# The tanh and last product of each convolution unit, issued behind the next unit's evictions

## The chip, the cores and the metric

The kernel runs on one core of a Trainium2 chip. A core has a matrix engine (TensorE, PE in the profile), three engines for elementwise work (VectorE or DVE, ScalarE or ACT, GpSimd or POOL) and SyncE (SP), which here only issues loads. Each engine works through its own list of instructions in order; an instruction whose input isn't there yet holds everything behind it on that engine. Matmul results land in PSUM, a small memory of eight buffers here, and another engine must read a result out (evict it) before the buffer can be used again. The metric is the time of one execution in microseconds (us) on the device; the median of several is compared.

## The reference

A trunk of two layers over x (1, 256, 1024). Each layer normalises x, multiplies it by one wide input matrix, feeds three token mixers (a Mamba-2 scan, attention over a sliding window, forgetting attention), projects each back to 1024, adds them with sigmoid gates, multiplies by an output matrix and adds x.

```python
for layer in range(DEPTH):                     # 2
    h = rms_norm(x, norm_w[layer])
    proj = einsum('bsd,de->bse', h, w_in[layer])        # 1024 x 12832
    (a_xbc, a_z, a_dt, b_q, b_k, b_v, b_z,
     c_q, c_k, c_v, c_f, c_z, gates) = split(proj, ...)
    y_a = mamba2_branch(a_xbc, a_z, a_dt, conv_w[layer], conv_b[layer], ...)
    y_b = sliding_window_branch(b_q, b_k, b_v, b_z, sinks[layer], cos, sin)
    y_c = forgetting_attention_branch(c_q, c_k, c_v, c_f, c_z, f_bias[layer])
    branch = einsum('bsiw,iwd->bsid', stack([y_a, y_b, y_c], axis=2), w_proj[layer])
    g = sigmoid(gates + gate_bias[layer])
    x = x + einsum('bsd,de->bse', sum(g * branch, axis=2), w_out[layer])
return rms_norm(x, final_norm_w)
```

The change touches the first lines of the Mamba-2 branch, a causal convolution of width 4 over each of 2048 channels by itself, followed by silu:

```python
xbc = silu(causal_depthwise_conv(a_xbc, conv_w, conv_b))
xs, bm, cm = split(xbc, [1024, 1536])          # inputs, B and C of the scan
```

## The kernel before

**Products.** Every large product is made in three: activations and weights are each split into a high and a low half, and hi·hi, lo·hi and hi·lo are summed in PSUM. Weights stream in over SyncE's DMA queue into six raw buffers (`load_part`, L331), ScalarE copies the high half out (L261) and VectorE subtracts it for the low half (L262). At most four split parts are held at a time, and a new part is split when an old one is released. So both engines have this stream of splits (276 of each in the kernel) beside everything else.

**Units.** The program is a list of operations, worked through one after the other. A unit is 24 matmuls into one of three PSUM buffers named mm: `chan` makes 128 channels x 256 tokens (24 matmuls, 128x256 each), `tok` 128 tokens x up to 512 columns. Five more PSUM buffers (mx) serve attention, scan and transposes. When a unit is done, its eviction reads the buffer; a later unit's first matmul needs the buffer that was evicted three units before.

**The convolution units.** `u_conv` (L672 to L694) handles 128 channels, unit u of 16: 8 to 11 are B, 12 to 15 are C, 0 to 7 are xs. ScalarE evicts the product twice, a plain copy to x_ (L682) and a scaled copy with bias to a (L683). VectorE adds the three shifted taps onto a (L686, 255, 254 and 253 wide). ScalarE then makes the tanh of a (L689), and VectorE the last product (th + 1) * a (L690), which by the scaling of the weights is the silu. After units 1, 3, 5 and 7 a group of the scan (`ssd_group`, L696) is queued. So a ScalarE instruction (the tanh) waits for VectorE's taps, and a VectorE instruction (the last product) for that tanh, within each unit.

**The order around it.** In each layer, the sixteen conv units come in pairs, 8 and 9 first, then up to 15, then 0 to 7, with other units between the pairs. Layer 0: gate-path units of the sliding-window branch (`u_z`, tanh L770, product L773) behind 9, 11 and 15; two gate units (`u_gate`, bias added L894, tanh L895) behind 3; behind 5 the *late split*, `split_late`, which splits the attention result times its gate path into the halves (L261 and L262) that the attention projection multiplies; and that projection's first units behind 7. Layer 1: `u_z` behind 9, 13 and 15, the two gate units behind 1, and behind 5 the late split directly followed by the projection. Between units, `pump` starts steps of what is queued (attention: scores and softmax L542, exp L548, L554 to L560, transposed probabilities L577; the scan: DMA of cumulated decays L701, L707, L714, L717, taps of the decay L724, their exps L726 and L730, L731, state L737, decay times scores L742), each with a due time on a clock that counts only matmuls.

PE's order is thus fixed by the program. VectorE, ScalarE and GpSimd get theirs in this part from a scheduler, which mostly keeps the order in which the program issues, and moves an instruction where it expects another to be ready sooner. Tiles of 128x256 (tag L1) have fourteen buffers.

Of the kernel before, what the change touches and what calls it, by code (L numbers as in the profile page):

```python
# [13 lines left out]
AF = mybir.ActivationFunctionType  # L14
ALU = mybir.AluOpType

P = 128
S = 256
# [7 lines left out]
D_K, D_Q, D_QK, D_G0, D_FOX, D_BDMA, D_BIAS = 6.0, 5.5, 2.0, 8.0, 0.0, 4.0, 2.0  # L26
# [18 lines left out]
def hybrid_trunk(  # L45
# [14 lines left out]
                bias=2, st=2, sm=6)  # L60
    count = [0]

    def T(tag, shape, dtype=F32, bufs=None):
        count[0] += 1
        return sb.tile(shape, dtype, tag=tag, name=f"{tag}_{count[0]}",
                       bufs=bufs if bufs is not None else BUFS.get(tag, 1))
# [8 lines left out]
    def pmx():  # L75
        return PS("mx", 5)

    act = nc.scalar.activation
    stt = nc.vector.scalar_tensor_tensor
# [19 lines left out]
    def transpose(o, a, i):  # L99
        clock["t"] += 0.109  # L100
        nc.tensor.transpose(o, a, i)  # L101

    def launch(br, gen, delay=0.0):
        clock["n"] += 1
        waiting.append([clock["t"] + delay, clock["n"], br, gen, None])
# [145 lines left out]
    def halves(ap):  # L251

        return ap.rearrange("p (a i) -> p a i", a=2)
# [142 lines left out]
    for l in range(L):  # L396
        y = Layer()
# [274 lines left out]
    def u_conv(y, u, c):  # L672
        def f(w):
            p = chan(y, w, c)
            if u == 8:
                y.bcT = T("L8", [P, 8, S])
            if u == 0:
                y.xs = T("L8", [P, 8, S])
            dst = y.xs[:, u, :] if u < 8 else y.bcT[:, u - 8, :]
            a = T("L1", [P, S])  # L680
            x_ = T("L1", [P, S])
            act(halves(x_), p, AF.Copy)  # L682
            act(halves(a), p, AF.Identity, scale=y.vec[:, 48 + u:49 + u], bias=y.vec[:, 64 + u:65 + u])  # L683
            for j in (2, 1, 0):
                s = 3 - j
                stt(a[:, s:S], x_[:, 0:S - s], y.vec[:, 16 * j + u:16 * j + u + 1], a[:, s:S],  # L686
                    op0=ALU.mult, op1=ALU.add)
            th = T("L1", [P, S])
            act(th, a, AF.Tanh)  # L689
            stt(dst, th, 1.0, a, op0=ALU.add, op1=ALU.mult)  # L690
            if u < 8 and u % 2 == 1:
                launch(0, ssd_group(y, u // 2), D_G0)
            pump()
        return f  # L694

    def ssd_group(y, g):  # L696
        yield lambda: not any(m[2] == 1 for m in waiting)
        yield "ssd"
        xdt = T("L2", [P, 2, 256])
        bcg = T("L4", [P, 4, S])  # L700
        nc.scalar.dma_start(bcg, y.cumd[4 * g:4 * g + 4, 0, :].partition_broadcast(P))  # L701
        hs = slice(4 * g, 4 * g + 4)
        for t in range(2):
            p = pmx()
            for j in range(2):
                transpose(p[:, j * P:(j + 1) * P], y.xs[:, 2 * g + j, t * P:(t + 1) * P], ident)
            tt(xdt[:, t, :].rearrange("p (h d) -> p h d", h=4),  # L707
               p[:, 0:256].rearrange("p (h d) -> p h d", h=4), bc(y.dt[:, t, hs], 2, 64), op=ALU.mult)
        p = pmx()
        transpose(p[:, 0:P], y.bcT[:, g, 0:P], ident)  # L710
        bt = T("bt", [P, P])
        act(bt, p[:, 0:P], AF.Copy)
        ds = T("ds", [P, 4], bufs=2)
        tt(ds, bcg[:, :, P - 1], y.acum[:, 0, hs], op=ALU.subtract)  # L714
        act(ds, ds, AF.Exp)
        xds = T("L1", [P, 256])
        tt(xds.rearrange("p (h d) -> p h d", h=4), xdt[:, 0, :].rearrange("p (h d) -> p h d", h=4),  # L717
           bc(ds, 2, 64), op=ALU.mult)
        decs = []
        for c in range(2):  # L720
            tk = slice(c * P, (c + 1) * P)
            dec = T("L2", [P, 4, P])
            for h in range(4):
                stt(dec[:, h, :], bcg[:, h, tk], y.acum[:, c, 4 * g + h:4 * g + h + 1], negtri,  # L724
                    op0=ALU.subtract, op1=ALU.add)
            act(dec, dec, AF.Exp)  # L726
            decs.append(dec)

        cx = T("L2", [P, 4, P])
        act(cx, bcg[:, :, P:S], AF.Exp)  # L730
        tt(cx, cx, bc(y.bcT[:, 4 + g, P:S], 1, 4), op=ALU.mult)  # L731
        yield D_SSD

        p = pmx()
        mm(p[:, 0:256], bt, xds, start=True, stop=True)
        st = T("st", [P, 256])
        act(st, p[:, 0:256], AF.Copy)  # L737
        for c in range(2):
            tk = slice(c * P, (c + 1) * P)
            p = pmx()  # L740
            mm(p[:, 0:P], y.bcT[:, g, tk], y.bcT[:, 4 + g, tk], start=True, stop=True)
            tt(decs[c], decs[c], bc(p[:, 0:P], 1, 4), op=ALU.mult)  # L742
        yield D_SSD2
        for c in range(2):
            tk = slice(c * P, (c + 1) * P)
            for j in range(2):
                u = 2 * g + j
                py = pmx()
                for s in range(c + 1):
                    for i in range(2):  # L750
                        h = 2 * j + i
                        hc = slice(64 * h, 64 * h + 64)
                        a, b = (xdt[:, c, hc], decs[c][:, h, :]) if s == 0 else (st[:, hc], cx[:, h, :])
                        mm(py[64 * i:64 * i + 64, 0:P], a, b, start=(s == 0), stop=(s == c))
                stt(y.xs[:, u, tk], y.xs[:, u, tk], y.dsk[:, u:u + 1], py[:, 0:P],
                    op0=ALU.mult, op1=ALU.add)
        yield D_EVAC
        tokens["ssd"] += 1


    def u_z(y, br, u, c):
        def f(w):
            p = chan(y, w, c)
            if u == 0 and br != 0:
                y.sz[br] = T("L8", [P, NK, S])
            if u == 0 and br == 0:
                y.yh[br] = T("L8", [P, 2, NK, P], F32R)
                y.yl[br] = T("L8", [P, 2, NK, P], F32R)
            th = T("L1", [P, S])
            act(halves(th), p, AF.Tanh, scale=0.5)  # L770
            y.zdone.add((br, u))
            if br != 0:
                stt(halves(y.sz[br][:, u, :]), halves(th), 1.0, p, op0=ALU.add, op1=ALU.mult)  # L773
            else:
                drain(0)
                sz = T("L1", [P, S])
                stt(halves(sz), halves(th), 1.0, p, op0=ALU.add, op1=ALU.mult)
                tt(y.xs[:, u, :], y.xs[:, u, :], sz, op=ALU.mult)
                sq = T("L1", [P, S])
                act(sq, y.xs[:, u, :], AF.Square)  # L780
                y.sq.append(sq)
                if u % 2 == 1:
                    tt(y.sq[-2], y.sq[-2], y.sq[-1], op=ALU.add)
                    launch(3 if u < 4 else 4, group_norm(y, u // 2, y.sq[-2]), D_GN1)
            pump()
        return f
# [28 lines left out]
    def u_cv(y, c, t, i=None):  # L815

        def f(w):
            p = tok(y.hTh, y.hTl, w, t)
            if y.cv is None:
                y.cv = T("L8", [P, 2, D])  # L820
            m = w.n if i is None else w.n - 16
            rn = 1.0 if y.rn is None else y.rn[:, t:t + 1]
            if i is None:
                act(halves(y.cv[:, t, c:c + m]), p, AF.Copy, scale=rn)
            else:
                n = w.n // 2
                act(y.cv[:, t, c:c + n], p[:, 0, :], AF.Copy, scale=rn)
                act(y.cv[:, t, c + n:c + m], p[:, 1, 0:m - n], AF.Copy, scale=rn)
                logits(y, t, i, p[:, 1, m - n:n])
            pump()  # L830
        return f

    def u_ck(y, j, c):
        def f(w):
            p = chan(y, w, c)
            y.ckT[j] = T("qt", [P, 2, S])
            act(halves(y.ckT[j][:, 0, :]), p, AF.Copy)
            if j % 2 == 0:
                launch(2, fox_quad(y, j), D_FOX)
            pump()  # L840
        return f
# [44 lines left out]
    def u_gate(y, br, c, t):  # L886

        def f(w):
            if t == 0:
                y.gb = T("L2", [P, 512])  # L890
                nc.scalar.dma_start(y.gb, gate_bias[y.l, br:br + 1, c:c + 512].to_broadcast([P, 512]))
            p = tok(y.hTh, y.hTl, w, t)
            g = T("L2", [P, 512])
            tt(halves(g), p, halves(y.gb), op=ALU.add)  # L894
            act(g, g, AF.Tanh, scale=0.5)  # L895
            y.gate[t] = g
            pump()
        return f
# [300 lines left out]
    with tc.manual_schedule(engines={ENG.PE, ENG.DVE, ENG.Activation, ENG.Pool}):  # L1199
# [11 lines left out]
        p = pmx()  # L1211
# [151 lines left out]
```

## Time and profile before

| | |
|---|---|
| time, median of 3 runs | 845.81 us (844.84 to 847.25) |
| the profiled execution | 846.9 us, of which the span is 845.2 |
| granted TensorE clock, mean | 0.996 |
| tanh L689 | 32 times, 417 ns each (13.4 us); ScalarE idle before it 46.5 us in 28 of them, ended by the taps L686 |
| last product L690 | 32 times, 420 ns each; VectorE idle before it 6.5 us in 12 of them, ended by L689 |
| taps L686 | 96, 478 ns each (45.9 us) |
| hi copies L261, 128x1024 | 276, 981 ns (266.3 us) |
| lo halves L262, 128x1024 | 276, 1159 ns (315.6 us) |
| conv units: first and last tanh | 80.2 and 598.6 us |

How to read it: a group's row gives the busy time of all its instructions, the mean of one, the time that its engine stood idle just before them, and what ended that. "[1.61 <-ACT L L683]" behind an instruction in the timeline means that its engine stood 1.61 us before it and that ScalarE's L683 ended the wait; timeline rows begin with the start and the duration in us, and "x2" marks two like instructions in one row. Names of engines: PE, PEld (its weight loads, which overlap it), DVE, ACT, POOL. The clock is the share of full speed that TensorE was granted.

### The profile page before, as it was taken

The numbers are of one execution on the slowest core, as the hardware profiler recorded it, in microseconds if no ns is written. First come the engines' busy times: TensorE is split into PE (matmuls) and PEld (weight loads), VectorE is DVE, ScalarE is ACT, GpSimd is POOL, SyncE is SP. The second block draws the span as 40 slices with busy tenths as digits, with TensorE's granted clock in tenths as the row PEclk, the third lists the DMA queues.
The fourth block names the chain that finished last, engine by engine and source line by source line (L and its number), as shares of the span: only waits on it lengthen the run. The fifth ranks groups of instructions, "written<-read, shape, count | busy, mean of one in ns | idle before, by whom it ended". The sixth has DMA issues, their size and how long they took to land.

```text
span 845.2 us, 16836 instructions
## 1 busy us (share of the span) xinstructions
PE 828.2 (98%) x6341; PEld 766.2 (91%) x6341; DVE 652.4 (77%) x1418; ACT 507.1 (60%) x1030; POOL 94.2 (11%) x149
## 2 busy tenths in 40 slices
PE   8999999999999999999999999998999999999996
PEld 7999988889999998888999999887899999988896
DVE  6978798898786778665778797988877767785665
ACT  7747667656666666353664676765556666654442
POOL 3330000000111011110005100000001110111000
PEclk9999999999999999999999999999999999999999
DMA  9967554577646556675687556645765565576632
GB/s 302 272 177 223 158 150 146 186 237 202 201 141 180 151 164 215 197 248 177 219 271 207 177 169 214 185 139 187 218 184 163 162 175 151 162 236 212 212 100 75
DMA packets 129563, 159.46 MB, mean 189 GB/s; under 512 B 7970, under 2 KB 98202, under 8 KB 129482
## 3 DMA queue, kind: packets, MB, share of 16 engines
q1 hardware_dynamic: 114960, 140.53, 55.1%
q10 hardware_dynamic: 13690, 16.24, 6.2%
q0 software_dynamic: 832, 1.62, 0.7%
q8 instruction: 50, 0.82, 0.4%
q14 instruction: 31, 0.25, 0.1%
HBM read 154.63 MB, written 2.16 MB: 186 GB/s over the span
## 4 chain that ended last, share of the span: by engine, by line
PE 72%; DVE 14%; ACT 6%; issue 3%; DMA 3%; POOL 0%; SPq 0%; ACTq 0%; POOLq 0%; DVEq 0%
PE mm L97 63%; PE mx L97 6%; DVE lo L262 5%; DVE L L686 3%; PE mx L101 2%; ACT hi L261 2%; DMA L<-cumd 2%; ACT pp L548 2%; DMA L<-in_x_dram 1%; DVE pp L560 1%; DVE L L690 1%; DVE L L262 1%; ACT L L577 1%; DVE pp L542 1%; DVE L L724 1%
## 5 line engine op out<-in xcount | busy, mean ns | idle before, releaser
L262 DVE TENSOR_TENSOR lo<-raw,hi 128x1024 fp32r<-128x1024 f32 (+2 forms) x276 | 315.6, 1159 | 85.1 <-ACT hi L261 78.7
L97 PE MATMUL mm<-L,hi 128*128 128x256 f32 x2112 | 373.2, 278 | 3.3 <-ACT L L683 1.6
L97 PEld LDWEIGHTS mm<-L,hi 128*128 128x128 f32 x2112 | 326.9, 192 | 11.8 <-issue 6.0
L261 ACT ACTIVATE hi<-raw 128x1024 fp32r<-128x1024 f32 (+2 forms) x276 | 266.3, 981 | 104.8 <-PE mm L97 85.5
L97 PE MATMUL mm<-hi,L 128*128 128x512 f32 (+2 forms) x1232 | 325.1, 352 | 3.0 <-DVE L L262 2.7
L97 PE MATMUL mm<-L,lo 128*128 128x256 f32 x1056 | 290.4, 275 | 0.0
L97 PEld LDWEIGHTS mm<-hi,L 128*128 128x128 f32 x1232 | 217.5, 190 | 27.3 <-DVE L L262 3.5
L97 PE MATMUL mm<-lo,L 128*128 128x512 f32 (+2 forms) x616 | 214.2, 349 | 0.0
L97 PEld LDWEIGHTS mm<-L,lo 128*128 128x128 f32 x1056 | 202.6, 192 | 0.1
L97 PEld LDWEIGHTS mm<-lo,L 128*128 128x128 f32 x616 | 116.7, 190 | 11.7
L864 POOL TENSOR_SCALAR_AFFINE_SELECT bias<-bias 128x128 f32<-128x128 f32 x64 | 29.5, 498 | 398.9 <-DMA bias<-cumd 381.5
L548 ACT ACTIVATE pp<-pp,nm 128x128 f32<-128x128 f32 (+1 forms) x128 | 56.6, 443 | 16.3 <-DVE nm L542 16.1
L686 DVE SCALAR_TENSOR_TENSOR L<-L,vec,L 128x255 f32<-128x255 f32 (+2 forms) x96 | 45.9, 478 | 2.0 <-ACT L L683 0.9
L689 ACT ACTIVATE L<-L 128x256 f32<-128x256 f32 x32 | 13.4, 417 | 46.5 <-DVE L L686 46.5
L560 DVE TENSOR_SCALAR pp<-pp,rsum 128x128 f32<-128x128 f32 (+1 forms) x128 | 32.2, 315 | 0.5
L770 ACT ACTIVATE L<-mm 128x256 f32<-128x256 f32 x48 | 17.9, 372 | 22.2 <-PE mm L97 18.1
L895 ACT ACTIVATE L<-L 128x512 f32<-128x512 f32 x24 | 15.1, 628 | 25.8 <-DVE L L894 25.5
L577 ACT ACTIVATE L<-mx 128x512 f32<-128x512 f32 x48 | 27.0, 595 | 1.8 <-PE mx L101 1.4
L101 PE MATMUL mx<-ident,pp 128*128 128x128 f32 x192 | 26.8, 275 | 0.0
L542 DVE CUSTOM_DVE_ANT_0 pp<-mx,wmask,nsink 128x128 f32<-128x128 f32 x64 | 23.9, 411 | 1.4 <-PE mx L97 1.4
L261 ACT ACTIVATE L<-L 128x512 fp32r<-128x512 f32 (+1 forms) x36 | 18.4, 531 | 10.8 <-DVE L L811 7.3
L894 DVE TENSOR_TENSOR L<-mm,L 128x512 f32<-128x512 f32 x24 | 16.4, 684 | 9.9 <-PE mm L97 9.9
(190 smaller groups left out, 719.5 us busy)
## 6 DMA issues: line engine op xcount, KB each, us to landing
raw<-in_w_in_dram SPq DMA_DIRECT2D x191, 512.0 KB, 4.6
raw<-in_w_proj_dram SPq DMA_DIRECT2D x48, 512.0 KB, 4.8
raw<-in_w_out_dram SPq DMA_DIRECT2D x16, 512.0 KB, 4.9
L<-cumd ACTq DMA_DIRECT2D x8, 512.0 KB, 6.2
bias<-cumd ACTq DMA_DIRECT2D x16, 256.0 KB, 4.0
L<-in_gate_bias_dram ACTq DMA_DIRECT2D x12, 256.0 KB, 5.3
raw<-in_w_in_dram SPq DMA_DIRECT2D x4, 408.0 KB, 3.5
raw<-in_w_in_dram SPq DMA_DIRECT2D x4, 384.0 KB, 4.9
```

Of the source, the lines that this page charges most:

```text
L97: nc.tensor.matmul(o, a, b, **kw)
L101: nc.tensor.transpose(o, a, i)
L261: keep(act)(hi, src, AF.Copy)
L262: keep(tt)(lo, src, hi.bitcast(F32), op=ALU.subtract)
L542: nc.vector.tensor_tensor_reduce(out=pp[:, i, sl], in0=score(p, i, b), in1=biases(p, i, b), scale=-0.125, scalar=1.0e30 if ns is None else ...
L548: act(pp[:, i, sl], pp[:, i, sl], AF.Exp, scale=-1.0, bias=nm[:, e:e + 1], accum_out=sums[:, e:e + 1])
L560: ts(pp[:, i, sl], pp[:, i, sl], rs[:, 2 * i + b:2 * i + b + 1], 0.5, op0=ALU.mult, op1=ALU.mult)
L577: act(pT, pt, AF.Copy)
L686: stt(a[:, s:S], x_[:, 0:S - s], y.vec[:, 16 * j + u:16 * j + u + 1], a[:, s:S], op0=ALU.mult, op1=ALU.add)
L770: act(halves(th), p, AF.Tanh, scale=0.5)
L864: nc.gpsimd.affine_select(out=bias[:, i, dst], in_=bias[:, i, src], compare_op=ALU.is_ge, fill=NEG, base=0, pattern=[[-1, P]], channel_mul ...
L894: tt(halves(g), p, halves(y.gb), op=ALU.add)
```

## The change

In `u_conv` the tanh and the last product (with the launch of the scan group that follows an odd unit) become a closure `end`, put on a list `ends_later`. A new function `finish` runs all pending closures; it is given an eviction and issues them under `tc.issue_after`, which places them behind that eviction in program order. `finish` is called behind the eviction of the next conv unit, or of a `u_z`, `u_cv`, `u_ck` or `u_gate` unit if that comes first. No instruction is added or removed.

```diff
@@ u_conv
-            act(halves(a), p, AF.Identity, scale=y.vec[:, 48 + u:49 + u], bias=y.vec[:, 64 + u:65 + u])
+            finish(act(halves(a), p, AF.Identity, scale=y.vec[:, 48 + u:49 + u], bias=y.vec[:, 64 + u:65 + u]))
             for j in (2, 1, 0):
                 s = 3 - j
                 stt(a[:, s:S], x_[:, 0:S - s], y.vec[:, 16 * j + u:16 * j + u + 1], a[:, s:S],
                     op0=ALU.mult, op1=ALU.add)
-            th = T("L1", [P, S])
-            act(th, a, AF.Tanh)
-            stt(dst, th, 1.0, a, op0=ALU.add, op1=ALU.mult)
-            if u < 8 and u % 2 == 1:
-                launch(0, ssd_group(y, u // 2), D_G0)
+            def end():
+                th = T("L1", [P, S])
+                act(th, a, AF.Tanh)
+                stt(dst, th, 1.0, a, op0=ALU.add, op1=ALU.mult)
+                if u < 8 and u % 2 == 1:
+                    launch(0, ssd_group(y, u // 2), D_G0)
+            ends_later.append(end)
             pump()
         return f
+    ends_later = []
+    def finish(out):
+        with tc.issue_after(out.ins):
+            while ends_later:
+                ends_later.pop(0)()
@@ u_z
-            act(halves(th), p, AF.Tanh, scale=0.5)
+            finish(act(halves(th), p, AF.Tanh, scale=0.5))
@@ u_cv
-                act(halves(y.cv[:, t, c:c + m]), p, AF.Copy, scale=rn)
+                finish(act(halves(y.cv[:, t, c:c + m]), p, AF.Copy, scale=rn))
@@ u_ck
-            act(halves(y.ckT[j][:, 0, :]), p, AF.Copy)
+            finish(act(halves(y.ckT[j][:, 0, :]), p, AF.Copy))
@@ u_gate
-            act(g, g, AF.Tanh, scale=0.5)
+            finish(act(g, g, AF.Tanh, scale=0.5))
```

The file grows by eleven lines, so that in the changed kernel the tanh is L690 and the last product L691, and lines behind them are 11 higher: L742 becomes L753, L724 becomes L735, L726 becomes L737. The orders of PE, GpSimd and SyncE are the same before and after, line numbers apart. ScalarE has 920 rows in both; VectorE has 1346 before and 1345 after, where two equal neighbours fell into one row. (Rows name line, operation, outputs <- inputs and size; a number behind a tile's name only tells tiles apart, and the two kernels count differently.)

ScalarE in layer 0, around units 13 and 14. Before (L_305 is a of unit 13, L_310 that of unit 14, the hi copies are of the weight stream):

```order
L682 ACTIVATE L_306_1744<-mm_1706 128x256
L683 ACTIVATE L_305_1743<-mm_1706,vec_862 128x256
L261 ACTIVATE hi_1811<-raw_1502 128x1024
L261 ACTIVATE hi_1829<-raw_1520 128x1024
L689 ACTIVATE L_307_1750<-L_305_1743 128x256
L682 ACTIVATE L_311_1789<-mm_1763 128x256
L683 ACTIVATE L_310_1788<-mm_1763,vec_862 128x256
L261 ACTIVATE hi_1896<-raw_1588 128x1024
```

After (L_304 is a of unit 13, L_309 that of unit 14; L_283 is a of unit 12):

```order
L682 ACTIVATE L_305_1741<-mm_1703 128x256
L683 ACTIVATE L_304_1740<-mm_1703,vec_862 128x256
L690 ACTIVATE L_306_1744<-L_283_1636 128x256
L261 ACTIVATE hi_1808<-raw_1499 128x1024
L261 ACTIVATE hi_1826<-raw_1517 128x1024
L682 ACTIVATE L_310_1786<-mm_1760 128x256
L683 ACTIVATE L_309_1785<-mm_1760,vec_862 128x256
L690 ACTIVATE L_311_1789<-L_304_1740 128x256
L261 ACTIVATE hi_1896<-raw_1588 128x1024
```

Unit 13's tanh stood ahead of unit 14's two evictions and now stands behind them; unit 12's has moved behind unit 13's evictions.

VectorE in layer 0, where the scan's second group of decay products (L742) meets the taps of units 6 and 7. Before (L_433 is a of unit 6, L_443 that of unit 7):

```order
L686 SCALAR_TENSOR_TENSOR L_433_2434<-L_434_2435,vec_862,L_433_2434 128x254
L714 TENSOR_TENSOR ds_2863<-L_522_2849,acum_1426 128x4
L262 TENSOR_TENSOR lo_2536<-raw_2255,hi_2535 128x1024
L686 SCALAR_TENSOR_TENSOR L_433_2434<-L_434_2435,vec_862,L_433_2434 128x253
L742 TENSOR_TENSOR L_417_2337<-L_417_2337,mx_2509 128x512
L690 SCALAR_TENSOR_TENSOR L_340_1959<-L_435_2441,L_433_2434 128x256
L742 TENSOR_TENSOR L_418_2343<-L_418_2343,mx_2512 128x512
L686 SCALAR_TENSOR_TENSOR L_443_2481<-L_444_2482,vec_862,L_443_2481 128x255
```

After (L_432 is a of unit 6, L_442 that of unit 7):

```order
L686 SCALAR_TENSOR_TENSOR L_432_2431<-L_433_2432,vec_862,L_432_2431 128x254
L262 TENSOR_TENSOR lo_2533<-raw_2255,hi_2532 128x1024
L691 SCALAR_TENSOR_TENSOR L_340_1959<-L_434_2435,L_426_2386 128x256
L686 SCALAR_TENSOR_TENSOR L_432_2431<-L_433_2432,vec_862,L_432_2431 128x253
L686 SCALAR_TENSOR_TENSOR L_442_2478<-L_443_2479,vec_862,L_442_2478 128x255
L262 TENSOR_TENSOR lo_2545<-raw_2267,hi_2544 128x1024
L691 SCALAR_TENSOR_TENSOR L_340_1959<-L_444_2482,L_432_2431 128x256
L686 SCALAR_TENSOR_TENSOR L_442_2478<-L_443_2479,vec_862,L_442_2478 128x254
L753 TENSOR_TENSOR L_416_2334<-L_416_2334,mx_2506 128x512
L686 SCALAR_TENSOR_TENSOR L_442_2478<-L_443_2479,vec_862,L_442_2478 128x253
L753 TENSOR_TENSOR L_417_2340<-L_417_2340,mx_2509 128x512
```

All three taps of unit 7 and a further lo half now stand ahead of the second decay product. On ScalarE at that place, unit 5's second eviction stands behind both decay exps in both orders.

VectorE in layer 1, up to the last lo half of the late split (its first input, L_1132, is the attention result times its gate path). Before (L_1405 is a of unit 7, L_1318 is xs):

```order
L724 SCALAR_TENSOR_TENSOR L_1395_7569<-L_1388_7550,acum_6658,negtri_79 128x128 x2
L717 TENSOR_TENSOR L_1394_7567<-L_1387_7549,ds_7564 128x256
L690 SCALAR_TENSOR_TENSOR L_1318_7191<-L_1385_7536,L_1383_7529 128x256
L724 SCALAR_TENSOR_TENSOR L_1395_7569<-L_1388_7550,acum_6658,negtri_79 128x128 x2
L724 SCALAR_TENSOR_TENSOR L_1396_7575<-L_1388_7550,acum_6658,negtri_79 128x128 x4
L686 SCALAR_TENSOR_TENSOR L_1405_7621<-L_1406_7622,vec_6094,L_1405_7621 128x255
L262 TENSOR_TENSOR L_1409_7632<-L_1132_6133,L_1408_7631 128x2x256
```

After (L_1404 is a of unit 7):

```order
L728 TENSOR_TENSOR L_1393_7564<-L_1386_7546,ds_7561 128x256
L735 SCALAR_TENSOR_TENSOR L_1394_7566<-L_1387_7547,acum_6658,negtri_79 128x128 x4
L735 SCALAR_TENSOR_TENSOR L_1395_7572<-L_1387_7547,acum_6658,negtri_79 128x128 x4
L742 TENSOR_TENSOR L_1396_7578<-L_1396_7578,L_1188_6459 128x512
L262 TENSOR_TENSOR L_1408_7629<-L_1132_6133,L_1407_7628 128x2x256
L686 SCALAR_TENSOR_TENSOR L_1404_7618<-L_1405_7619,vec_6094,L_1404_7618 128x255
L691 SCALAR_TENSOR_TENSOR L_1318_7191<-L_1406_7622,L_1382_7526 128x256
```

The last product and the tap of unit 7 that stood ahead of the lo half now stand behind it, and the scan's product that was L731 (now L742) stands ahead of it.

More of the change, by code (lines that the diff above doesn't have):

```diff
@@ L827, in f @@
                 act(y.cv[:, t, c:c + n], p[:, 0, :], AF.Copy, scale=rn)
-                act(y.cv[:, t, c + n:c + m], p[:, 1, 0:m - n], AF.Copy, scale=rn)
+                finish(act(y.cv[:, t, c + n:c + m], p[:, 1, 0:m - n], AF.Copy, scale=rn))
                 logits(y, t, i, p[:, 1, m - n:n])
```

## The prediction

> **What bounds the kernel now.** I read the page's first part, then the busy time of stretches, then who TensorE (PE) waited for, then the single waits in the timeline.
>
> ```profile
> PE 828.2 (98%) x6341; PEld 766.2 (91%) x6341; DVE 652.4 (77%) x1418; ACT 507.1 (60%) x1030; POOL 94.2 (11%) x149
> 100.00:130.00 30.00, 27.67 (x264) 26.23 (x263) 24.62 (x64) 18.74 (x49) 1.59 (x4) 1.00 0.59 177
> ...
> 570.00:600.00 30.00, 27.29 (x170) 24.17 (x169) 26.64 (x55) 16.64 (x30) 1.42 (x4) 0.94 0.63 194
> ```
>
> PE is busy 828.2 of 845.2 us. Only some 17 us can be won at all, and only where PE stands still. Two stretches with conv units do show that (in each row the numbers are length, PE, weight load, VectorE, ScalarE, GpSimd, clock): 100 to 130 in layer 0 and 570 to 600 in layer 1, the second with a granted clock of 0.94. These are PE's waits from 100 to 176, and from 503 to 592:
>
> ```profile
> PE mm L97 <- ACT L L683: 1.6, 1, 1.6
> PE mm L97 <- DVE L L773: 0.7, 1, 0.7
> PE mx L97 <- ACT L L577: 0.4, 1, 0.4
> PE mx L97 <- DVE L L742: 0.2, 1, 0.2
> ...
> PE mm L97 <- DVE L L262: 2.7, 1, 2.7
> PE mm L97 <- DVE L L773: 0.5, 1, 0.5
> PE mm L97 <- DVE L L894: 0.5, 1, 0.5
> ```
>
> That is 2.9 us in layer 0 and 3.7 in layer 1. ScalarE's 46.5 us in front of the tanh (table above) are no gain by themselves: most of that is covered by PE's three product buffers.
>
> **What the change takes away.** The largest wait of layer 0, and what ScalarE and VectorE did around it:
>
> ```profile
> 119.31 0.28 PE L97 MATMUL mm<-L,hi 128*128 128x256 f32 x1
> 121.19 0.38 PE L97 MATMUL mm<-L,hi 128*128 128x256 f32 x1 [1.61 <-ACT L L683]
> ...
> 116.16 2.00 ACT L261 ACTIVATE hi<-raw 128x1024 fp32r<-128x1024 f32 x2
> 119.99 0.42 ACT L689 ACTIVATE L<-L 128x256 f32<-128x256 f32 x1 [1.84 <-DVE L L686]
> 120.32 0.37 ACT L682 ACTIVATE L<-mm 128x256 f32<-128x256 f32 x1
> ...
> 110.98 0.42 DVE L690 SCALAR_TENSOR_TENSOR L<-L,L 128x256 f32<-128x256 f32 x1 [0.55 <-ACT L L689]
> 111.33 0.34 DVE L542 CUSTOM_DVE_ANT_0 pp<-mx,wmask,nsink 128x128 f32<-128x128 f32 x1
> ```
>
> The two hi copies end at 118.1. ScalarE then stands 1.84 us before unit 13's tanh, and the evictions of unit 14 (0.37 and about 0.5 us) follow it. In the new order (first pair of rows above) they follow the hi copies directly: the buffer is free at 118.1 + 0.8 = 118.9, and PE asks at 119.4. The 1.6 us go even if nothing else moves. Next in line is unit 15's eviction, which now also has no tanh of its own pair ahead of it.
>
> The second saving is on VectorE: the last product no longer stands right behind its own tanh. At 111 it waited 0.55 us and held the softmax (L542) behind it. The waits of VectorE from 90 to 176, and from 502 to 578:
>
> ```profile
> DVE lo L262 <- ACT hi L261: 4.6, 6, 1.6
> DVE L L690 <- ACT L L689: 3.3, 6, 0.5
> ...
> DVE lo L262 <- ACT hi L261: 3.4, 5, 1.6
> DVE L L690 <- ACT L L689: 2.7, 5, 0.5
> ```
>
> Of layer 0's six waits on the tanh, five lie after 104 and before the second gate unit at 158: 5 x 0.55 = 2.7 us. Of the 4.6 us behind hi copies I count 0.8, since the longest (1.6) sits behind a gate's tanh, which stays. VectorE's head start at 158 is then 3.5 us; the bounds are 0 (everything comes back as other waits) and 2.7 + 4.6 = 7.3. I take the value near the rows on the tanh. In layer 1 four of the five waits lie before the second gate unit at 563: 2.2 us, and 0.9 of the 3.4: 3.1; bounds 0 and 5.6. With such a lead the waits on L773, L577 and L894 (0.7, 0.4, 0.5, 0.5 us) go too, because each is a VectorE or ScalarE step that was late by less than the lead.
>
> **What it adds.** No instruction is added; PE's, GpSimd's and SyncE's orders stay as they were, and ScalarE keeps its 920 rows. But the order on VectorE puts more ahead of the scan's two decay products (L742), which PE needs:
>
> ```profile
> 171.65 1.22 DVE L262 TENSOR_TENSOR lo<-raw,hi 128x1024 fp32r<-128x1024 f32 x1
> 172.79 0.48 DVE L686 SCALAR_TENSOR_TENSOR L<-L,vec,L 128x253 f32<-128x253 f32 x1
> 173.18 0.68 DVE L742 TENSOR_TENSOR L<-L,mx 128x512 f32<-128x512 f32 x1
> 173.80 0.43 DVE L690 SCALAR_TENSOR_TENSOR L<-L,L 128x256 f32<-128x256 f32 x1
> 174.15 0.68 DVE L742 TENSOR_TENSOR L<-L,mx 128x512 f32<-128x512 f32 x1
> 174.74 0.48 DVE L686 SCALAR_TENSOR_TENSOR L<-L,vec,L 128x255 f32<-128x255 f32 x1
> ...
> 174.97 0.44 PE L97 MATMUL mx<-L,L 128*64 128x128 f32 x4 [0.16 <-DVE L L742]
> ```
>
> From start to start an L262 takes 1.14 us, an L686 0.39. Between the gate unit and the second L742 the new order has all three taps of unit 7 (3 x 0.39 = 1.2) and one more L262 (1.1) ahead, and one L714 of 128x4 less (I put it at under 0.1): 2.2 us. PE already waited 0.2 us here, so there is no cover: of the 2.9 us of layer 0, PE keeps only 3.5 - 2.2 = **1.3 us**; bounds -2.2 (no head start) and +2.9.
>
> Layer 1. PE stops in the first unit of the attention projection, at its 20th matmul, which needs the last lo half of the late split:
>
> ```profile
> 565.03 1.52 DVE L686 SCALAR_TENSOR_TENSOR L<-L,vec,L 128x255 f32<-128x255 f32 x3 [0.29 <-ACT L L683]
> 566.95 1.23 DVE L262 TENSOR_TENSOR lo<-raw,hi 128x1024 fp32r<-128x1024 f32 x1 [0.40 <-ACT hi L261]
> 571.49 0.42 DVE L690 SCALAR_TENSOR_TENSOR L<-L,L 128x256 f32<-128x256 f32 x1 [0.54 <-ACT L L689]
> 577.58 0.68 DVE L262 TENSOR_TENSOR L<-L,L 128x512 fp32r<-128x512 f32 x1
> ...
> 575.22 0.38 PE L97 MATMUL mm<-hi,L 128*128 128x512 f32 x1
> 578.31 0.80 PE L97 MATMUL mm<-hi,L 128*128 128x512 f32 x1 [2.71 <-DVE L L262]
> 578.89 0.63 PE L97 MATMUL mm<-lo,L 128*128 128x512 f32 x1
> 579.32 1.06 PE L97 MATMUL mm<-hi,L 128*128 128x512 f32 x2
> ...
> 581.76 0.38 PE L97 MATMUL mm<-hi,L 128*128 128x512 f32 x1
> ```
>
> Between 565.0 and that lo half the new order drops one L690 and one L686 and adds one L731 of the scan (128x512, at an L742's 0.62 from start to start), about -0.1; the three waits marked in the rows (1.2 us) go. So the lo half ends at 578.2 - 1.3 = 576.9 with no head start, at 573.8 with 3.1. PE comes 1.0 us earlier (the two 0.5s), so it asks at 574.4. The wait is gone, with 0.6 us to spare; without the hi copies' part of the lead (2.2 in all) 0.3 us would stay. All 3.7 us of layer 1 are won.
>
> And one thing more. After the 2.71 us the matmuls come at 0.43 us (578.89 to 579.32), where they came at 0.22 before: half clock, until about 581.7. By the stretch's clock that is 30 x (1.00 - 0.94) = 1.8 us; I take 1.7, half of 578.31 to 581.76. After the 1.61 us at 121 the clock in the row of 100 to 130 is 1.00. So an idle of 2.7 us costs it and one of 1.6 does not. Layer 1 gives 3.7 + 1.7 = **5.4 us**.
>
> The Trainium skill (TensorE: Matmul & The Clock Gate, "HAM oscillation — how this bites in real kernels") says that only idle gaps over about 3.4 us throw the array back to half clock, judged in a free-running window. By that rule 2.71 us would not do it; the row at 578.89 says that here it did, and the row decides.
>
> **The sum.** 1.3 + 5.4 = 6.7 us. The profiled execution took 846.9 (span 845.2 and 1.7 around it), 1.1 above the median of 845.8, so 840.2 for such an execution and 845.8 - 6.7 = **839.1** for the median. If everything goes, and about 1 us of restarts between matmuls with it, 2.9 + 3.7 + 1.7 + 1 = 9.3: 836.5.
>
> **The rivals.** A difference under 0.3% (2.5 us) is about what a measurement of this kernel can't tell from none.
>
> *No head start (0.17).* VectorE is busy 24.6 of 30 us from 100 to 130, and its work is the same; removed waits may return as waits on hi copies, two of which now stand behind a tanh at the gates. Then layer 0 gains nothing; in layer 1 the lo half comes at 576.9 instead of 578.2 and the clock still halves: 1.3 us, 844.5. Against it: the 0.55 us waits are pure round trips with work behind them.
>
> *Half of it (0.08).* Layer 0 gives nothing (1.7 - 2.2 is below nothing, offset by the 1.6 us that go anyway), and in layer 1 the lo half comes at 575.4, PE idles 1.0 us, the clock stays: 578.3 - 575.5 + 1.7 = 4.5 us, 841.3.
>
> *The clock does not follow the wait (0.08).* Only the free-running window's position made the clock fall in this execution, and the timed ones mostly lack it. Then 1.3 + 3.7 = 5.0: 840.8. That is what the Trainium skill's window rule, named above, would make of it; one profile can't exclude it.
>
> *Slower: the scan holds PE (0.07).* Layer 0 shows a second coupling:
>
> ```profile
> 163.84 0.56 ACT L683 ACTIVATE L<-mm,vec 128x256 f32<-128x256 f32 x1
> ...
> 165.41 0.60 PE L97 MATMUL mm<-hi,L 128*128 128x512 f32 x2
> ```
>
> Unit 5's second eviction frees the buffer of the projection at 165.41. Now both exps of the decays (L726), which wait for VectorE's L724s, stand ahead of it, and the projection's products, weights and the scan's L742 behind. Without a head start the buffer is free about 0.7 us late and the second L742 2.2 us late; if such a stop also halves the clock (1.7, as after 2.71), layer 0 loses 3.9 and layer 1 wins 1.3: 845.8 + 2.6 = 848.4. It decides once VectorE's lead at 158 is near nothing. Against it: five round trips of 0.55 us are gone by then.
>
> *Forecast (0.60).* 836.5 to 842.
>
> That the tanh doesn't move is excluded by the new order's rows.
>
> **The numbers.** Faster by over 0.3%: 0.60 + 0.08 + 0.08 = 0.76. Within: 0.17. Slower: 0.07. The range starts at the bound where all waits go, 836.4, and reaches into the no-head-start case, to 844.0; left out are the slower case and the rest of that one.
>
> **What would show it.** Right: PE's 1.6 us on L683 and 2.7 on the late split's lo are gone, the clock of 570 to 600 is near 1.00, VectorE's waits on the tanh fall from 6.0 us in these stretches to under 2, and the largest wait left near 173 is on the decay products, 1 to 2 us. Wrong: a PE wait on the late split above 2 us with a clock below 0.97 there; PE waiting over 1 us on unit 5's eviction; no wait on the decay products at all (then layer 0 gives up to 2.9).

## The result and the profile after

| | before | after |
|---|---|---|
| median (range) | 845.45 us (844.84 to 847.25, 4 executions) | 841.29 us (840.92 to 841.78, 4 executions) |
| profiled execution, span | 846.9, 845.2 | 841.54, 839.8 |
| ratio, 95% interval | | 0.9948 (0.993 to 0.9965) |

The change makes the kernel 4.2 us faster by the medians; 6.7 were forecast. (The two profiled executions differ by 5.4 us, in part because that of before is one in which the clock fell.) In the later comparisons the kernel before ran 45 more times, with medians of 846.3 to 846.5; what spreads it is told below under the longer wait.

The first part of the page of the changed kernel, then its stretches that answer to those of the prediction (length, PE, weight load, VectorE, ScalarE, GpSimd, clock):

```profile
PE 826.3 (98%) x6341; PEld 765.8 (91%) x6341; DVE 651.7 (78%) x1418; ACT 507.9 (60%) x1030; POOL 99.7 (12%) x149
100.00:130.00 30.00, 29.54 (x301) 27.98 (x300) 25.54 (x65) 20.21 (x51) 1.54 (x4) 1.00 0.59 181
160.00:190.00 30.00, 28.07 (x161) 24.34 (x160) 27.30 (x57) 19.74 (x33) 5.56 (x4) 1.00 0.62 200
570.00:600.00 30.00, 28.24 (x175) 25.06 (x175) 28.40 (x59) 19.58 (x32) 1.24 (x4) 1.00 0.57 190
```

The two stretches that were open before are fuller, and the clock of 570 to 600 is 1.00. But 160 to 190, where PE was busy 29.84 of 30 us before, is down to 28.07. PE's waits from 60 to 600 say why:

```profile
PE mm L97 <- DVE L L262: 1.8, 1, 1.8
PE mx L97 <- DVE L L753: 1.1, 2, 0.7
PE mm L97 <- ACT L L683: 0.8, 1, 0.8
PE mm L97 <- DVE L L784: 0.5, 1, 0.5
```

The 1.6 us near 121 are gone. The late split (L262) still holds PE for 1.8 us; the 0.8 on L683 are new, and so are the 1.1 on the decay products (0.2 before). PE's matmuls stand in the same order in both traces, so the start of the n-th one before less that after is the time won up to there. Without the 0.3 us by which the first 30 us differ it grows to 1.8 us at the matmul at 121 and 2.7 at 155, falls back to 0.6 at 175, is 0.8 at 500, 2.5 at 564, 3.5 behind the late split and 5.1 once the half clock of before is over, where it stays. Layer 0 thus gave 0.6 us, layer 1 4.3, and 0.2 came between.

**Where layer 0 lost it again.** PE, and ScalarE around it:

```profile
163.45 0.70 PE L97 MATMUL mm<-hi,L 128*128 128x512 f32 x2 [0.84 <-ACT L L683]
173.03 0.66 PE L97 MATMUL mx<-L,L 128*64 128x128 f32 x8 [0.66 <-DVE L L753]
174.12 0.44 PE L97 MATMUL mx<-L,L 128*64 128x128 f32 x4 [0.43 <-DVE L L753]
...
161.26 0.63 ACT L737 ACTIVATE L<-L 128x512 f32<-128x512 f32 x1 [0.33 <-DVE L L735]
161.80 0.37 ACT L682 ACTIVATE L<-mm 128x256 f32<-128x256 f32 x1
162.32 0.63 ACT L737 ACTIVATE L<-L 128x512 f32<-128x512 f32 x1
162.85 0.55 ACT L683 ACTIVATE L<-mm,vec 128x256 f32<-128x256 f32 x1
```

Unit 5's second eviction (162.85) stands behind both exps of the decays (L737), and the attention projection waits for the buffer. The section on the change says that this was so in both orders. That is wrong; before, both evictions stood ahead of the exps:

```profile
163.57 0.36 ACT L682 ACTIVATE L<-mm 128x256 f32<-128x256 f32 x1
163.84 0.56 ACT L683 ACTIVATE L<-mm,vec 128x256 f32<-128x256 f32 x1
164.63 0.65 ACT L726 ACTIVATE L<-L 128x512 f32<-128x512 f32 x1 [0.24 <-DVE L L724]
165.17 0.63 ACT L730 ACTIVATE L<-L 128x512 f32<-128x512 f32 x1
165.78 0.63 ACT L726 ACTIVATE L<-L 128x512 f32<-128x512 f32 x1
```

The prediction ("now both exps stand ahead of it") has it right.

**Where VectorE's head start in layer 1 went.** First before, then after, VectorE near 511 and at the second gate unit:

```profile
510.33 0.42 DVE L690 SCALAR_TENSOR_TENSOR L<-L,L 128x256 f32<-128x256 f32 x1 [0.55 <-ACT L L689]
511.28 1.23 DVE L262 TENSOR_TENSOR lo<-raw,hi 128x1024 fp32r<-128x1024 f32 x1 [0.52 <-ACT hi L261]
514.65 0.16 DVE L714 TENSOR_TENSOR ds<-L,acum 128x4 f32<-128x4 f32 x1 [1.75 <-DMA L<-cumd]
515.13 1.22 DVE L262 TENSOR_TENSOR lo<-raw,hi 128x1024 fp32r<-128x1024 f32 x1
...
563.52 1.22 DVE L262 TENSOR_TENSOR lo<-raw,hi 128x1024 fp32r<-128x1024 f32 x1
```

```profile
508.51 1.22 DVE L262 TENSOR_TENSOR lo<-raw,hi 128x1024 fp32r<-128x1024 f32 x1
513.64 0.16 DVE L725 TENSOR_TENSOR ds<-L,acum 128x4 f32<-128x4 f32 x1 [2.96 <-DMA L<-cumd]
514.12 1.22 DVE L262 TENSOR_TENSOR lo<-raw,hi 128x1024 fp32r<-128x1024 f32 x1
...
555.44 0.42 DVE L691 SCALAR_TENSOR_TENSOR L<-L,L 128x256 f32<-128x256 f32 x1 [1.00 <-ACT L L690]
560.51 1.22 DVE L262 TENSOR_TENSOR lo<-raw,hi 128x1024 fp32r<-128x1024 f32 x1
```

The first lo half comes 2.8 us earlier than before (511.28 to 508.51), the one behind the small subtraction only 1.0 (515.13 to 514.12), which is PE's own 1.1. In between VectorE waits for a DMA, 1.75 us before and 2.96 after: the lead is paid back in full. Behind that wait a new lead grows, to 1.9 us at 563.52 (3.0 less the 1.1). This `ds` belongs to the scan, some fifty microseconds on; the scheduler has moved it here, because it needs nothing but its DMA, and everything on VectorE stands behind it. In layer 0 the same wait grew from 2.7 to 3.8 us.

### The profile page after: what moved, and what is told of

Read it like the earlier page. It is cut to its first block, busy times and chain, and to the rows that moved or that the text cites. A ratio compares the mean times of both kernels' runs of the same rounds, so it can differ in the third digit from the quotient of the medians.

```text
span 839.8 us, 16828 instructions
## 1 busy us (share of the span) xinstructions
PE 826.3 (98%) x6341; PEld 765.8 (91%) x6341; DVE 651.7 (78%) x1418; ACT 507.9 (60%) x1030; POOL 99.7 (12%) x149
## 4 chain that ended last, share of the span: by engine, by line
PE 81%; DVE 9%; ACT 4%; issue 2%; DMA 2%; POOL 0%; SPq 0%; POOLq 0%; ACTq 0%; DVEq 0%
PE mm L97 71%; PE mx L97 7%; DVE lo L262 3%; PE mx L101 3%; DVE L L686 2%; ACT pp L548 2%; ACT hi L261 1%; DMA L<-cumd 1%; DMA L<-in_x_dram 1%; DVE L L735 0%; ACT L L577 0%; DVE L L691 0%; DVE pp L560 0%; DVE L L788 0%; DVE L L590 0%
## 5 line engine op out<-in xcount | busy, mean ns | idle before, releaser
L262 DVE TENSOR_TENSOR lo<-raw,hi 128x1024 fp32r<-128x1024 f32 (+2 forms) x276 | 315.7, 1159 | 80.8 <-ACT hi L261 74.2
L875 POOL TENSOR_SCALAR_AFFINE_SELECT bias<-bias 128x128 f32<-128x128 f32 x64 | 33.9, 566 | 389.0 <-DMA bias<-cumd 259.8
L686 DVE SCALAR_TENSOR_TENSOR L<-L,vec,L 128x253 f32<-128x253 f32 (+2 forms) x96 | 45.4, 478 | 1.4 <-ACT L L683 0.6
L690 ACT ACTIVATE L<-L 128x256 f32<-128x256 f32 x32 | 13.2, 414 | 18.3 <-DVE L L686 18.3
```

The source lines that it names most:

```text
L262: keep(tt)(lo, src, hi.bitcast(F32), op=ALU.subtract)
L875: nc.gpsimd.affine_select(out=bias[:, i, dst], in_=bias[:, i, src], compare_op=ALU.is_ge, fill=NEG, base=0, pattern=[[-1, P]], channel_mul ...
```

## The experiments

The ratios are to the kernel before, run beside each. Time won within a trace is always PE's n-th matmul against that of the profiled execution before.

**Layer 1 alone** (`if y.l == 1: ends_later.append(end)`, else `end()` at once).

> The ends are deferred in layer 1 alone; layer 0 is as before. Theory (layer 1 carries the gain; in layer 0 what PE wins up to 155 us is given back between 163 and 174 us, at unit 5's eviction and at the scan's decay products): 4.2 us of layer 1 stay and 0.5 to 0.7 us go, about 841.8 us beside 845.4 before; PE waits 1.6 us on L683 near 121 and under 0.3 us on the decay products, and the late split's wait stays near 1.8 us. Rival (both layers give alike, since the same pairs are moved): about 843.3 us.

842.37 us (840.80 to 845.53, 6 executions), ratio 0.9956 (0.994 to 0.9973). The time lies between the two, but the kernel before took 846.5 us beside it, and by the ratio it is the theory's (841.8 of 845.4 is 0.9957, 843.3 is 0.9975). The trace has the waits of the theory: 1.9 us on L683 near 121, 0.2 on the decay products, 2.0 on the late split, and PE wins 1.7 us from 500 to the late split, as with the whole change. The profiled execution is the slowest of the six, and its clock halved twice, at 123.6 and at 577.6.

**Only the last product deferred.**

```diff
+            th = T("L1", [P, S])
+            act(th, a, AF.Tanh)
             def end():
-                th = T("L1", [P, S])
-                act(th, a, AF.Tanh)
                 stt(dst, th, 1.0, a, op0=ALU.add, op1=ALU.mult)
```

> Only the last product is deferred; the tanh stays in its own unit, ahead of the next unit's evictions on ScalarE. Theory (VectorE's lead comes from the round trips on the tanh, 0.54 us each, whatever the tanh's own place): PE's 1.6 us on L683 near 121 stay, VectorE's waits on the tanh fall from 6.0 to under 2 us in the two layers, the late split's wait falls to 1 to 2 us and the clock of 570 to 600 is 1.00; 840.5 to 842.5 us. Rival (the gain is that ScalarE no longer stands before a tanh with evictions behind it): no gain here, 844.5 to 845.5 us, with a wait on the late split of over 2.4 us and a clock below 0.97.

847.43 us, ratio 1.0013 (1.0003 to 1.0024): no gain. VectorE's waits on the tanh from 90 to 176 and 502 to 578 are what they were:

```profile
DVE L L692 <- ACT L L689: 3.3, 6, 0.5
...
DVE L L692 <- ACT L L689: 2.7, 5, 0.5
```

The reason is that this run hardly changes what VectorE does, so it doesn't test the theory. In the scheduler's order 23 of the 32 last products have as many other instructions ahead of them on VectorE as before, among them all twelve that wait for the tanh (in the changed kernel only three of the 32 do). The wait and the softmax behind it, which the prediction shows at 110.98 and 111.33, are still there:

```profile
110.35 0.42 DVE L692 SCALAR_TENSOR_TENSOR L<-L,L 128x256 f32<-128x256 f32 x1 [0.54 <-ACT L L689]
110.69 0.34 DVE L542 CUSTOM_DVE_ANT_0 pp<-mx,wmask,nsink 128x128 f32<-128x128 f32 x1
```

ScalarE's order is that of before in nearly every place too. Of the rival's signs the wait on the late split is there (3.3 us), the clock below 0.97 is not. What the run shows is that with the tanh in its own unit, deferring the product in the program moves none of the products that wait. Whether the gain of the change comes from the tanh's place on ScalarE or from the product's on VectorE isn't separated by any run here.

**Units 4 to 7 of layer 0 in place** (`if y.l == 1 or u > 7 or u < 4: ends_later.append(end)`).

> As the changed kernel, but units 4 to 7 of layer 0 keep their tanh and last product in place. Theory (their deferral is what makes PE wait 0.84 us on unit 5's eviction, behind the decay exps, and 1.1 us on the decay products): both waits fall under 0.3 us each, and about 2 us come on top of the change: 839.3 us. Rival (VectorE has simply no lead at 158 us, so that the scan's products come as late in any order): 841.0 to 841.5 us, with 1.5 us or more of waits left there.

839.39 us, ratio 0.9915 (0.9902 to 0.9928). From 60 to 200 PE has one wait left:

```profile
PE mx L97 <- DVE L L756: 0.2, 1, 0.2
```

As the theory had it: the new order around the scan cost about 2 us.

**The pending end ahead of the gate's tanh** (`finish(tt(halves(g), p, halves(y.gb), op=ALU.add))` instead of `finish(act(g, ...))`).

> As the changed kernel, but the pending end is placed behind the gate unit's bias addition instead of its tanh, so that the tanh of the conv unit stands ahead of the gate's tanh on ScalarE and no longer between it and the next hi copies. Theory (the gate's tanh waits for VectorE's addition, and VectorE then waits 1.0 us for the conv tanh queued behind it; but the hi copies that follow are only 0.3 us late by it): VectorE's 1.0 us waits on the tanh near 152 and 555 go, the late split's wait falls by about 0.3 us to 1.5, 840.7 to 841.1 us. Rival (the 1.0 us are on the way to the late split's last lo half): its wait falls to 0.8, 840.2 us or less.

840.30 us, ratio 0.9928 (0.9915 to 0.9941). VectorE's waits on the tanh from 90 to 176 fall from 1.4 to 0.4 us, and the late split's wait is 1.4, as the theory had it; the time is a little under its range.

**Both of these together.**

> The scan units of layer 0 in place (as in the third run) and the ends ahead of the gates' tanh (as in the fourth) together. Theory (the two costs lie in different places, so they add: about 2 us in layer 0, 0.3 to 0.8 us at the gates): 838.4 to 839.0 us, the late split's wait 1.4 us. Rival (the lead won in one place is used up in the other): no better than the third run, 839.4 us.

837.77 us, ratio 0.9902 (0.9889 to 0.9915), better than the theory; the late split's wait isn't 1.4 us but gone. The order there is that of the run before. What differs is the DMA: VectorE waited 1.3 and 0.4 us for it in layer 1, against 3.1 there. With like orders in layer 1 it lands at different times in the two traces, and the late split follows it. That led to the last three runs.

**The projection of layer 1 behind unit 7**, on top of both (`lights = {..., 6: [split_late], 7: [gp.pop(0)]}`).

> As the run before, and in layer 1 the attention projection's first units stand behind unit 7, as they do in layer 0, with the late split where it was. Theory (the 1.4 to 1.8 us that PE still waits for the late split's last lo half are due to the projection coming too early for VectorE, and two conv units of PE work cover them): the wait goes, 837.0 to 837.6 us. Rival (VectorE is then late for what follows, the evictions of units 6 and 7 and the scan's decay products, and the wait only moves): 838.5 us or more, with over 1 us of PE waits on other lines between 570 and 600 us.

838.87 us, ratio 0.9917 (0.9905 to 0.993). No wait on the late split, and over 60 to 600 none above 0.4 us, but no gain on the run before either. The theory's waits are right, its time isn't: the trace of the run before has no wait on the late split left that this could save.

**Two units later** (`finish` in `u_conv` leaves one end pending).

> As the changed kernel, but the tanh and last product follow the evictions of the second next conv unit instead of the next (other units still end all that is pending). Theory (what ScalarE's idle time before the tanh costs is only the evictions queued behind it, and one unit of distance has already freed those): no more gain, 840.8 to 841.8 us, although ScalarE's idle time before the tanh falls from 18.3 us to under 10. Rival (that idle time is a cost by itself): 840 us or less.

839.09 us, ratio 0.9921 (0.9909 to 0.9932): the rival's side. ScalarE's idle time before the tanh fell from 18.3 to 10.9 us, and the late split's wait is gone. But VectorE's order moved as well, the last products of units 4 and 5 among others to other places around the late split, so it isn't shown that the idle time itself was the cost.

**A longer wait.**

```diff
             split(y.yh[br][:, :, u:u + 2, :], y.yl[br][:, :, u:u + 2, :], ...)
+        if br == 1 and y.l == 1:
+            for _ in range(1):
+                tt(y.yl[br][:, :, u:u + 2, :], ..., op=ALU.subtract)     # the last lo half again
```

> As the changed kernel, but the lo half that PE waits for in layer 1 is computed twice, the second time some 1.7 us later, so that PE's wait grows from 1.8 to about 3.5 us. Theory (the clock is judged in fixed windows of 3.41 us, and halves for one window when PE idled through more than half of the one before; so a wait of 1.7 to 3.4 us halves it in some executions and a longer one in all): mean clock at most 0.997 in every execution, 1.7 us of wait and 1.7 us of half clock more than the changed kernel, about 844.7 us. Rival (the clock falls by chance, whatever the wait): some executions keep 0.998 or more, and the time is 843.0 us in those.

846.50 us, ratio 1.0003 (0.9993 to 1.0014); PE's wait is 3.7 us in the profile. The mean clock is at most 0.997 in 11 of 12 executions and 0.999 in one (844.39 us, the fastest): nearly the theory, but not in every one, and the median is 1.8 us above the theory's 844.7. With the wait of 1.8 us of the changed kernel it was 0.998 or 0.999 in all four. The kernel before has 0.997 or less in 25 of its 45 executions (median 846.7 us) and 0.998 in 20 (845.7). The mean clock is a rough sign only: the run with the subtraction held, below, has 0.997 without a fall between 60 and 600 us. The traces bear out windows. The first three rows are of before, where PE stood 2.71 us up to 578.3; the next two of the product-only run, where it stood 3.32 us up to 578.85:

```profile
574.80:578.20 3.40, 0.80 (x4) 0.37 (x2) 3.40 (x12) 3.17 (x7) 1.42 (x4) 1.00 0.00 0
578.20:581.60 3.40, 3.29 (x8) 2.66 (x9) 3.40 (x6) 0.66 (x2) 0.00 (x0) 0.50 0.69 212
581.60:585.00 3.40, 3.40 (x19) 3.04 (x18) 1.68 (x5) 1.30 (x3) 0.00 (x0) 1.00 0.80 261
```

```profile
573.80:577.20 3.40, 1.73 (x9) 1.16 (x7) 3.40 (x13) 2.88 (x7) 1.27 (x4) 1.00 0.14 50
577.20:580.60 3.40, 1.75 (x8) 1.57 (x9) 3.40 (x6) 1.27 (x2) 0.00 (x0) 1.00 0.69 179
```

The 3.32 us kept the clock, since they fell half into one window and half into the next, and PE was busy for just over half of each. In the first run (layer 1 alone) 1.94 us were enough, in one window (busy 1.47 of 3.40), and so were the 1.96 us up to 576.86, ahead of the fall at 577.6:

```profile
120.20:123.60 3.40, 1.47 (x13) 1.42 (x13) 3.33 (x7) 2.61 (x5) 0.00 (x0) 1.00 0.55 152
123.60:127.00 3.40, 3.40 (x18) 3.40 (x17) 3.37 (x6) 1.95 (x5) 0.00 (x0) 0.51 0.79 188
```

**The small subtraction held at its place**, on the changed kernel, on the kernel with both corrections, and on the kernel before (`pin` keeps an instruction in program order).

```diff
-        tt(ds, bcg[:, :, P - 1], y.acum[:, 0, hs], op=ALU.subtract)
+        pin(tt)(ds, bcg[:, :, P - 1], y.acum[:, 0, hs], op=ALU.subtract)
```

> As the changed kernel, but the scan's small subtraction (128x4, L725), which the scheduler had moved far ahead in VectorE's order, to the middle of the conv units, where it waits for its DMA (3.8 us near 98 and 3.0 near 511), is held at its place in the program. Theory (VectorE's lead is given back at this wait, which ends when the DMA lands, however early VectorE comes): the two waits go, the lead reaches the late split, whose wait of 1.8 us goes in the profile, and so does the 0.5 us on the gate path's product near 126; 838.7 to 839.5 us. Rival (VectorE then waits in the same stretch for evictions and hi copies, which come from PE and ScalarE): 840.8 us or more, the late split's wait still over 1.4 us.

> The scan units of layer 0 in place, the ends ahead of the gates' tanh, and the small subtraction held at its place. Theory (what was left were executions in which the DMA landed late): 836.4 to 837.2 us, no PE wait over 0.3 us from 100 to 180 and from 500 to 600. Rival (nothing is left to win there): 837.6 to 838.0 us as in the run with the first two.

> The kernel before, with nothing deferred, and only the small subtraction held at its place. Theory (VectorE's wait on the DMA, 2.7 and 1.8 us, made the late split late before the change too): the late split's wait falls from 2.7 us to about 1, below what halves the clock, and the 1.6 us on L683 near 121 stay or grow: 842.5 to 843.5 us. Rival (the round trips on the tanh and the hi copies use up the time, since each unit's tanh still stands ahead of the next evictions): 845 us or more.

835.58 us on the changed kernel, ratio 0.9871 (0.9855 to 0.9888), and 835.58 with both corrections too, 0.9872 (0.9856 to 0.9889). VectorE and PE of the first, PE with a 0.3 us wait left from 60 to 600, and VectorE's waits from 500 to 578, in which no DMA appears:

```profile
PE mx L97 <- DVE L L794: 0.3, 1, 0.3
...
DVE lo L262 <- ACT hi L261: 2.3, 4, 0.8
DVE L L691 <- ACT L L690: 1.2, 2, 1.0
DVE L L686 <- ACT L L683: 0.9, 2, 0.6
```

```profile
100.00:130.00 30.00, 30.00 (x306) 28.47 (x305) 26.12 (x65) 22.58 (x53) 1.03 (x4) 1.00 0.67 198
570.00:600.00 30.00, 30.00 (x187) 26.99 (x186) 27.88 (x49) 16.78 (x27) 0.00 (x0) 1.00 0.73 225
```

PE doesn't stop in either stretch. The theory's waits hold, and the time is 3 us under its range: the waits around the scan in layer 0 went as well, with the deferral of units 4 to 7 in place, and the two corrections add nothing to that (the expectation for all three together has its waits right, its time not; 835.58 is under both of its ranges).

Not all of this is the lead, for with the subtraction held the scheduler makes another order. In layer 0 unit 5's second eviction (159.66) now stands ahead of the second decay exp (160.11), and one lo half less stands ahead of the second decay product (169.62). So whether a lead alone would pay for the changed kernel's order there isn't shown. In layer 1 the late split's last lo half stands ahead of the scan's product L742 (0.6 us). It ends 5.7 us earlier than in the changed kernel (568.81 for 574.49), and PE needs it at 569.2; with 0.6 us more ahead of it about 0.3 us of wait would stay, by estimate, of 1.8. There it is the lead that counts.

The kernel before, with nothing deferred, takes 840.53 us with that one line, ratio 0.9933 (0.9917 to 0.9949): about as much as the whole change. There theory and rival were both off: the 1.6 us near 121 are gone, the 2.7 us on the late split stay,

```profile
PE mm L97 <- DVE L L262: 2.7, 1, 2.7
PE mx L97 <- ACT L L577: 0.4, 1, 0.4
```

and VectorE's waits on the tanh are the old 3.3 and 2.7 us. Part of what this run gains is the clock: its 2.68 us of wait fell into two windows (PE idle 1.0 and 1.6 us), and the profile has no fall, which is worth 1.6 us against that of before. From there the change is worth 4.95 us (840.53 to 835.58, two runs beside each other).

## Why the prediction was right and where it was off

- **The evictions behind the tanh.** The 1.6 us near 121 went, with 1.8 won at that matmul. Right, though the last run shows a second way: VectorE's taps come earlier without the DMA wait, and then the tanh isn't late either. The wait had two causes, and either removed it.
- **Head start, layer 0.** 3.5 us forecast at 158, 2.7 measured (VectorE's lo half at 158.64 came at 155.68, less the 0.3 at the start). The parts differ from the count: from 104 to 158 the waits on the tanh fell from 2.7 to 1.4 us and not to nothing, since a new one of 1.0 us stands behind the second gate's tanh (150.12), and those on hi copies fell from 4.1 to 3.0, where 0.8 was counted.
- **The cost of the new order, layer 0.** 2.2 us forecast, 2.1 measured, but not as it was reasoned: 1.1 at unit 5's eviction and 1.0 on the decay products, by PE's matmuls. The eviction was weighed only within the slower rival, as a matter of no lead; it belonged in the sum. Layer 0 gave 0.6 for 1.3.
- **Head start, layer 1: the step that failed.** "In layer 1 four of the five waits lie before the second gate unit at 563: 2.2 us, and 0.9 of the 3.4: 3.1." One of those tanh waits (0.55 at 510.33) and one hi wait (0.52 at 511.28) lie ahead of the DMA wait at 514.65, and what is won ahead of it is lost at it. 3.1 less 1.1 is 2.0; measured 1.9. That this agrees so well is partly luck: behind the DMA wait the waits on the tanh fell only from 1.6 to 1.4 us, again for a new 1.0 behind the gate's tanh (555.44), those on hi copies from 2.5 to 1.6, and those of the taps from 0.7 to 0.2. In layer 0 the count began behind the DMA wait, at 104; in layer 1 it did not. That this wait takes the lead is shown by holding the subtraction in place, where the late split's wait goes (but for some 0.3 us, which the other order may cover).
- **The late split.** Three waits (1.2 us) were to go; two of them, 0.29 on an eviction and 0.40 on a hi copy, are there after as before. And PE asked 1.7 us earlier, not 1.0: each of the two waits of 0.5 us was worth 0.7 to 0.8 by PE's matmuls. The prediction has such restarts between matmuls only in the bound, as "about 1 us", from no row. So 1.8 us of wait stayed instead of none.
- **The clock.** 1.7 us forecast, 1.6 in the profile. But the reason given, that an idle of 2.7 us costs it and one of 1.6 does not, is too simple: 3.32 us did not, and 1.94 did. The rival that the window's position decides was right in its mechanism; what it expected of it, that the timed executions of before mostly lack the fall, holds in 20 of 45. The Trainium skill (TensorE: Matmul & The Clock Gate, "HAM oscillation — how this bites in real kernels") sets the bound at gaps over about 3.4 us; the traces agree with the window, not with the bound: 1.94 us within one window halved it.
- **The slower rival** named the right place, unit 5's eviction (0.8 us of wait), but without its price: the clock didn't fall there.
- **The rival *Half of it*** fits the result best. It put layer 0 at nothing, layer 1 at 4.5 us and the time at 841.3, with the clock kept; the traces show 0.6 and 4.3, the time is 841.29. Only its idle of 1.0 us was 1.8. So the time fell into the forecast's range, which reaches to 842, while the head start that the sum rests on did not come in full.
- **The signs.** VectorE's waits on the tanh fell from 6.0 to 2.6 us, not to under 2, and the wait on the late split stayed at 1.8, between the sign of right (gone) and that of wrong (above 2). The 1.6 us on L683, the clock and the decay products (1.1 us in all) came as said.

## What to carry to other kernels

A lead on an engine is worth only as far as its next wait for something that doesn't move with it; before summing saved waits, mark the DMA landings in that engine's order and count only what lies between the last one and the place where the lead is spent. Look for small instructions that a scheduler has moved far ahead because all they need is a DMA: in an in-order queue one 128x4 subtraction held the whole engine for 1.8 to 3.8 us, and one line put it right for as much as the whole change. When instructions are deferred past the next evictions, compare the orders of every engine at the places where another branch joins, since a new order there can give back what was won. And before an experiment's time is read, see whether the edit reached the engine's order at all: a scheduler can leave an instruction where it was.

## What the runs showed of the hardware

The clock falls for one stretch of 3.4 us, and the stretches lie on a fixed grid: every fall between 60 and 600 us of the traces lasts 3.413 us in the clock's record, and the two of the first run begin 454.0 us apart (123.6 and 577.6), which is 133 such stretches. In this part of the traces PE was idle for 1.9 us or more of the window ahead of each fall, and where it was idle for 1.7 or less of each window (3.32 us over two of them, and the changed kernel's 1.76) the clock stayed. So where a wait lies on the grid decides whether it halves the clock. With a wait of some 2.7 us this would give the kernel before two kinds of execution, which its mean clocks bear out (medians 846.7 and 845.7 us, about 1 us of its spread); the wait itself was traced in one of them only.
